# Splitting fp32 weights by whole 128x2048 buffers in a two-layer decoder trunk

## The chip, the cores and the metric

One core of one Trainium2 chip runs the kernel in a single launch. The metric is device time in microseconds. The engines are called as in the profile: PE is TensorE, DVE is VectorE, ACT is ScalarE, POOL is GpSimd, SP is SyncE; PEld is TensorE's weight load, and a trailing q (SPq, ACTq, POOLq) names the queue on which an engine issues DMAs.

## The reference

A decoder trunk of two layers on 256 tokens of width 1024, all in fp32. Each layer is

```python
h = h + 0.5 * swiglu(rmsnorm(h, ffn1_norm[i]), ffn1_w_gate[i], ffn1_w_up[i], ffn1_w_down[i])   # hidden 2816
h = h + mixer_i(rmsnorm(h, mix_norm[i]))      # layer 0: differential attention, layer 1: Mamba-2 SSD
h = h + memory_cross_attention(rmsnorm(h, xa_norm[i]), mem, xa_mem_norm[i], xa_w_q[i], xa_w_kv[i], xa_w_o[i])
h = h + 0.5 * swiglu(rmsnorm(h, ffn2_norm[i]), ffn2_w_gate[i], ffn2_w_up[i], ffn2_w_down[i])
...
def swiglu(h, w_gate, w_up, w_down):
    return (jax.nn.silu(h @ w_gate) * (h @ w_up)) @ w_down
```

and a last RMSNorm follows. The memory of the cross-attention is 256 tokens of width 1024, normalised and projected anew in each layer. There are four FFNs, and with the projections of the mixers and the cross-attention nearly all the work is products of 256 tokens with weight matrices that are read once from DRAM.

## The kernel before, in words

**Products in three parts.** An fp32 product runs as three TensorE products of a reduced type, fp32r. Each operand is split into a high part (the value cast to fp32r) and a low part (value minus high part), and `mm3` adds x_hi·w_hi (line 262), x_hi·w_lo (263) and x_lo·w_hi (264) into one PSUM bank. For a weight the high part `whi` is a cast on ACT (line 224) and the low part `wlo` a subtract on DVE (line 225), which needs whi. So the first matmul on a piece of weight can go when the cast is done, the second when the subtract is done.

**Weights.** A class `W` loads 1 MB, four k-tiles of 128 rows by 512 columns (128x2048 in SBUF), by one DMA on SP's queue (line 161) into the pool `wp` of eight buffers. `Pair` (line 176) does so for two matrices side by side. `Sum` forms the sum of two weight tiles in place: on DVE (line 203), or by an accumulating DMA that POOL issues (line 199).

**Granules.** A `Gran` is the part of such a buffer that is split at once: two k-tiles of 512 columns, that is one half of a buffer, 128x1024. Its whi and wlo come from the pool `hp`, four buffers of 1024 each. `ready` and `use` split granules in the order in which PE will use them, two ahead (`AHEAD`) of the one in use; a buffer in hp is free when the matmuls on its granule are done.

**Units, sevens and hosts.** `wide` makes a unit that multiplies all 1024 rows with a block of 512 columns, in four granules. `stream` gives the same as single steps. `seven` multiplies a 2x2 arrangement of weight tiles with seven products in place of eight, after Strassen; four of the seven are on sums of weight tiles (x1 to x4) with sums of activations (`s_hi`, `s_lo`). Each of the seven has two granules of six matmuls each. In `ffn_hidden` the remaining steps (`gate`, `up`, `gateup`, `down`'s `out`) are hosts; `share` puts them between the seven products by a list of counts: so many hosts ahead of the first product, so many ahead of the second, and so on. `weave` makes one unit of it.

**Order.** The first two units, the first `gate` and the first `up`, are written out by hand for PE, DVE, ACT and SP, as is PE's order in the SSD stage. Elsewhere a scheduler orders the instructions of each engine. `Pipe` holds work with a due time in microseconds of PE's work (`pipe.after(us, f)`), and issues it when PE's program has come so far.

**Small work.** `gs` is silu of gate times up: ACT at line 787, DVE at line 804. `turn` transposes it (`htp`) and splits it into `hid_hi` (ACT, 857) and `hid_lo` (DVE, 858), the activations of `down`. Results of a seven are copied from PSUM as `p` (ACT, 823). During the first FFN DVE also works out the rope tables (`rope_tables`, lines 735 to 763) in small operations of 64 columns.

**Memory.** `mem` is loaded and normalised once in the first FFN, transposed on PE, and kept in SBUF as `memt`, eight tiles of 128x256. For each layer `MemKV.prep` scales and splits it into `mh` and `ml` (lines 457 and 459), and `MemKV.mix` makes the scaled tiles `my` (line 1074), from which `combine` forms the sums for the sevens of the value projection. Layer 1's preparation falls into the end of the SSD stage, whose output y is scaled, transposed (`ty`) and split into `y_hi` on ACT.

Of the kernel before, what the change touches and what calls it, by code (L numbers as in the profile page):

```python
# [57 lines left out]
def trunk(ctx, tc, a, out):  # L58
# [1 line left out]


    const = ctx.enter_context(tc.tile_pool(name="const", bufs=1))
    wp = ctx.enter_context(tc.tile_pool(name="wp", bufs=8))
    hp = ctx.enter_context(tc.tile_pool(name="hp", bufs=4))
    xp = ctx.enter_context(tc.tile_pool(name="xp", bufs=8))
    sp = ctx.enter_context(tc.tile_pool(name="sp", bufs=28))
    wk = ctx.enter_context(tc.tile_pool(name="wk", bufs=7))
# [4 lines left out]
    def slot(name, dt=F32):  # L72
        return sp.tile([P, 512], dt, name=name, tag="s")
# [4 lines left out]
    def small_ps(name):  # L78
        return pacc.tile([P, 512], F32, name=name, tag="acc")
# [28 lines left out]
    class Pipe:  # L108
        def __init__(self):
            self.t = 0.0  # L110
            self.q = []
# [93 lines left out]
    class Gran:  # L205


        def __init__(self, k0, nk, *parts, eng=None):
            self.k0, self.nk, self.parts, self.eng = k0, nk, parts, eng or nc.vector
            self.hi = None  # L210

        def split(self):
            if self.hi is not None:
                return
            hi = hp.tile([P, 1024], F32R, name="whi", tag="hi")
            lo = hp.tile([P, 1024], F32R, name="wlo", tag="lo")
            ncol = sum(n for _, _, n in self.parts)
            self.hi, self.lo = (t[:, :self.nk * ncol].rearrange("p (k c) -> p k c", c=ncol) for t in (hi, lo))
            o = 0
            for w, c0, n in self.parts:  # L220
                w.load()
                src = w.t[:, self.k0 - w.k0:self.k0 - w.k0 + self.nk, c0:c0 + n]
                hv = self.hi[:, :, o:o + n]
                nc.scalar.copy(hv, src)  # L224
                self.eng.tensor_tensor(self.lo[:, :, o:o + n], src, hv.bitcast(F32), op=ALU.subtract)  # L225
                o += n

    grans = []
# [12 lines left out]
            yield g  # L241

    def run_units():
        for gs, _ in units:
            for g in gs:
                g.at = len(grans)
                grans.append(g)
        E = mybir.EngineType
        with tc.manual_schedule(engines={E.PE, E.DVE, E.Activation, E.SP}):
            begin(first_norm)  # L250
            for gs, f in units[:2]:
                f(*gs)
        for gs, f in units[2:written[0]]:
            f(*gs)
        with tc.manual_schedule(engines={E.PE}):
            for gs, f in units[written[0]:written[1]]:
                f(*gs)
        for gs, f in units[written[1]:]:
            f(*gs)
# [316 lines left out]
    def v2(t, j=2):  # L576
        return t.rearrange("p (j t) -> p j t", j=j)
# [67 lines left out]
    lqk2 = lqk  # L645
    lqk = lqk.rearrange("p (k d) -> p k d", k=4)
    subln = cols0[:, KT:KT + 1]
    memt = [const.tile([P, S], F32, name=f"mem{j}") for j in range(KT)]
    mcol = const.tile([P, 16], F32, name="mcol")
    mnat = [[None, None], [None, None]]  # L650
    cols1 = const.tile([P, P], F32, name="cols1")
# [36 lines left out]
    def mem_prep():  # L688
# [12 lines left out]
        def turn(j):  # L701
            ps = small_ps("tin")
            for t in range(2):
                nc.tensor.transpose(ps[:, t * P:(t + 1) * P], mnat[t][j // 4][:, (j % 4) * P:(j % 4 + 1) * P], ident)
            nc.scalar.copy(memt[j], ps[:, :S])
        for j in range(KT):
            pipe.after(6.0 + 1.0 * j, lambda j=j: turn(j))


    def mem_stage():  # L710
# [67 lines left out]
    def ffn_hidden(nm, l, norm, fin, tail, extra=None):  # L778
# [95 lines left out]

        def part(half, ps):
# [181 lines left out]
    class MemKV:  # L1057


        def __init__(self, l):  # L1060
# [4 lines left out]
            self.x = []  # L1065
            self.s = [None] * 4

        def mix(self):
            y = [slot("my") for _ in range(KT // 2)]

            def full(p):
                for j in range(2):
                    k = 2 * p + j
                    nc.scalar.activation(v2(y[p])[:, j, :], memt[k], AF.Copy, scale=self.g[:, k:k + 1])
            for p in range(KT // 2):
                pipe.after(1.4 * p, lambda p=p: full(p))
            combine(y, self.s, [7.0 + 1.6 * i for i in range(8)])

        def k_split(self, c):
            self.ks[c] = split2(self.k[c], "mk")  # L1080

        def prep(self):
            self.x.clear()
            for j in range(KT):
                if j % 2 == 0:
                    mh, ml = slot("mh", F32R), slot("ml", F32R)
                xh, xl = (m[:, j % 2 * S:(j % 2 + 1) * S] for m in (mh, ml))
                split_act(xh, xl, memt[j], self.g[:, j:j + 1])
                self.x.append((xh, xl))

        def k_units(self, then=None, cs=(0, 2)):
            def fin(c):
# [584 lines left out]
```

## Time and profile before

| | us |
|---|---|
| median of 3 runs | 1260.77 |
| lowest, highest | 1260.51, 1260.87 |
| the profiled execution | 1260.69 |
| its span, first to last instruction | 1258.9 |

Mean granted TensorE clock 0.998. The rows below show one execution. A line of the timeline gives the start in us from the span's begin, the duration, the engine, the source line, the operation, out<-in, the shapes and the count, and in brackets the engine's idle time ahead of it and who ended it. Where a row stands for several instructions (x2, x4), its duration is that of all. The duration of a queued instruction overlaps with that of the one behind it, so what an instruction takes from an engine is read from the starts.

### The profile page before, as it was taken

The page shows a single profiled execution, that of the slowest core. Times are in us where ns is not written, and L with a number is a line of the kernel's source. Part 1 is how long each engine was busy: PE and PEld are TensorE (multiplying, and loading weights), DVE is VectorE, ACT ScalarE, POOL GpSimd, SP SyncE. Part 2 cuts the span into 40 slices and gives each one's busy share as a digit, 9 for nine tenths or more (in the row PEclk, how much of TensorE's full clock was granted, in tenths as well). Part 3 has the DMA queues.
Part 4 walks back from the last instruction along what each step waited for, and adds up shares of the span by engine and source line. Part 5 has one row for each costly group of instructions (what it writes and reads, how often), then busy time and mean ns, then how long its engine had stood idle before and what let it go on. Part 6 is the DMA issues. An engine that isn't in the chain of part 4 may idle for free.

```text
span 1258.9 us, 18179 instructions
## 1 busy us (share of the span) xinstructions
PE 1248.6 (99%) x6751; PEld 1070.7 (85%) x6751; DVE 1056.7 (84%) x1451; ACT 878.0 (70%) x1395; POOL 161.7 (13%) x139
## 2 busy tenths in 40 slices
PE   9999999999999999999999999999999999999997
PEld 6887888788998888888888889999998898888886
DVE  6988867887787998988898976788899887899886
ACT  6676764676676876767776756777777775877673
POOL 1101002201101011101111000022232100011100
PEclk9999999999999999999999999999999999999999
DMA  9979975345776698985899966665634786489961
GB/s 335 281 205 283 319 240 183 118 144 150 209 226 168 168 264 270 267 268 167 219 273 265 289 228 214 205 186 168 201 135 135 189 245 177 159 235 276 261 215 34
DMA packets 158316, 269.79 MB, mean 214 GB/s; under 512 B 6890, under 2 KB 43411, under 8 KB 158227
## 3 DMA queue, kind: packets, MB, share of 16 engines
q1 hardware_dynamic: 137744, 229.75, 53.6%
q0 software_dynamic: 19744, 38.28, 17.8%
q8 instruction: 53, 0.87, 0.3%
q10 hardware_dynamic: 738, 0.59, 0.1%
q14 instruction: 37, 0.30, 0.1%
HBM read 267.52 MB, written 1.08 MB: 213 GB/s over the span
## 4 chain that ended last, share of the span: by engine, by line
PE 91%; DVE 4%; DMA 2%; ACT 1%; issue 1%; POOL 0%; POOLq 0%; DVEq 0%; ACTq 0%
PE out L263 9%; PE out L264 8%; PE out L262 8%; PE seven L264 8%; PE seven L263 8%; PE seven L262 8%; DVE wlo L225 2%; PE xs L264 2%; PE xs L262 1%; PE xs L263 1%; DMA w<-in_ffn_w_gate_dram 1%; PE up L263 1%; PE up L264 1%; PE up L262 1%; PE htp L854 1%; PE mk L262 1%
## 5 line engine op out<-in xcount | busy, mean ns | idle before, releaser
L225 DVE TENSOR_TENSOR wlo<-w,whi 128x1024 fp32r<-128x1024 f32 (+2 forms) x532 | 641.0, 1219 | 136.2 <-ACT whi L224 126.7
L224 ACT CAST whi<-w 128x1024 fp32r<-128x1024 f32 (+2 forms) x534 | 552.3, 1040 | 261.9 <-PE out L264 102.5
L262 PE MATMUL out<-whi,hid_hi 128*128 128x512 f32 x336 | 131.4, 394 | 0.5 <-ACT whi L224 0.5
L263 PE MATMUL out<-wlo,hid_hi 128*128 128x512 f32 x336 | 131.3, 391 | 0.4 <-DVE wlo L225 0.3
L264 PE MATMUL out<-whi,hid_lo 128*128 128x512 f32 x336 | 131.0, 390 | 0.0
L262 PE MATMUL seven<-whi,s_hi 128*128 128x512 f32 x272 | 107.7, 396 | 0.4 <-ACT p L823 0.4
L263 PE MATMUL seven<-wlo,s_hi 128*128 128x512 f32 x272 | 106.1, 390 | 0.0
L264 PE MATMUL seven<-whi,s_lo 128*128 128x512 f32 x272 | 106.1, 390 | 0.0
L203 DVE TENSOR_TENSOR w<-w 128x2048 f32<-128x2048 f32 x32 | 73.2, 2286 | 5.7 <-DMA w<-in_ffn_w_gate_dram 5.6
L199 POOL DMA_DIRECT2D w<-in_ffn_w_up_dram x30 | 36.5, 1241 | 310.5 <-DVE wlo L225 273.7
L263 PEld LDWEIGHTS out<-wlo,hid_hi 128*128 128x128 f32 x336 | 63.2, 188 | 14.7 <-DVE wlo L225 2.1
L262 PEld LDWEIGHTS out<-whi,hid_hi 128*128 128x128 f32 x336 | 63.0, 188 | 13.3 <-ACT whi L224 0.8
L264 PEld LDWEIGHTS out<-whi,hid_lo 128*128 128x128 f32 x336 | 63.1, 188 | 13.2
L262 PE MATMUL seven<-whi,xh 128*128 128x512 f32 x180 | 70.1, 389 | 0.0
L264 PE MATMUL seven<-whi,xl 128*128 128x512 f32 x180 | 70.0, 389 | 0.0
L263 PE MATMUL seven<-wlo,xh 128*128 128x512 f32 x180 | 70.0, 389 | 0.0
L199 POOL DMA_DIRECT2D w<-in_ffn_w_gate_dram x30 | 36.9, 1467 | 221.7 <-DVE w L203 76.2
L264 PEld LDWEIGHTS seven<-whi,s_lo 128*128 128x128 f32 x272 | 51.1, 188 | 10.8
L262 PEld LDWEIGHTS seven<-whi,s_hi 128*128 128x128 f32 x272 | 51.1, 188 | 10.5 <-ACT p L823 0.8
L263 PEld LDWEIGHTS seven<-wlo,s_hi 128*128 128x128 f32 x272 | 51.1, 188 | 9.7
L262 PEld LDWEIGHTS seven<-whi,xh 128*128 128x128 f32 x180 | 33.8, 188 | 7.1
L263 PEld LDWEIGHTS seven<-wlo,xh 128*128 128x128 f32 x180 | 33.8, 188 | 7.1
(398 smaller groups left out, 3018.4 us busy)
## 6 DMA issues: line engine op xcount, KB each, us to landing
w<-in_ffn_w_up_dram SPq DMA_DIRECT2D x40, 1024.0 KB, 7.2
w<-in_ffn_w_down_dram SPq DMA_DIRECT2D x40, 1024.0 KB, 8.6
w<-in_ffn_w_gate_dram SPq DMA_DIRECT2D x38, 1024.0 KB, 7.1
w<-in_ssd_w_in_dram SPq DMA_DIRECT2D x24, 1024.0 KB, 5.4
w<-in_xa_w_kv_dram SPq DMA_DIRECT2D x16, 1024.0 KB, 5.1
w<-in_ffn_w_gate_dram POOLq DMA_DIRECT2D x30, 512.0 KB, 9.1
w<-in_ffn_w_up_dram POOLq DMA_DIRECT2D x30, 512.0 KB, 7.4
w<-in_da_w_in_dram SPq DMA_DIRECT2D x12, 1024.0 KB, 5.2
```

Of the source, the lines that this page charges most:

```text
L199: nc.gpsimd.dma_start(self.t[:, k:k + 2, :], w.src[r0:r0 + 2 * P, w.c0:w.c0 + w.n] .rearrange("(k p) c -> p k c", p=P), accum_op=ALU.add)
L203: nc.vector.tensor_tensor(self.t, self.l.t, w.t, op=ALU.add)
L224: nc.scalar.copy(hv, src)
L225: self.eng.tensor_tensor(self.lo[:, :, o:o + n], src, hv.bitcast(F32), op=ALU.subtract)
L262: nc.tensor.matmul(o, lhsT=lh, rhs=rh, start=start, stop=False, skip_group_check=onto)
L263: nc.tensor.matmul(o, lhsT=lh, rhs=rl, start=False, stop=False, skip_group_check=onto)
L264: nc.tensor.matmul(o, lhsT=ll, rhs=rh, start=False, stop=stop, skip_group_check=onto)
L854: nc.tensor.transpose(tp[:, j, t * P:(t + 1) * P], us[t][:, (i + j) * P:(i + j + 1) * P], ident)
```

## The change

Four edits go together.

- **Whole buffers.** `Group` joins granules. Two neighbouring halves of a whole 512-column buffer are split by one cast of 128x2048 (new line 252) and one subtract of 128x2048 (new line 253); the two granules then are views of the pair. Other granules of one unit share a buffer of 2048 but are split one by one as before (new lines 265 and 266). Of 520 splits of 128x1024, 430 become 215 pairs and 90 stay.
- **Pools.** hp has three buffers of 2048 each for whi and for wlo in place of four of 1024. wp has seven buffers in place of eight.
- **Counts.** Hosts stand between the seven products in twos, as whole pairs. In the first FFN the counts for its three column blocks change as the diff shows; in the others, five of the seven products stand in a row at the seam of two blocks.
- **Memory in DRAM.** `memt` is a DRAM tile. Two transposed tiles at a time are copied to SBUF and written by a DMA on ACT's queue. `prep` and `mix` each read four times 256 KB back on ACT's queue ahead of use (`fetch`, new line 1120); the scaling in `mix` starts 5 us later, that in `prep` 4 us later, and the sums in `mix` 5 us later.

```diff
-    wp = ctx.enter_context(tc.tile_pool(name="wp", bufs=8))
-    hp = ctx.enter_context(tc.tile_pool(name="hp", bufs=4))
+    wp = ctx.enter_context(tc.tile_pool(name="wp", bufs=7))
+    hp = ctx.enter_context(tc.tile_pool(name="hp", bufs=3))
...
+        def whole(self, other):
+            w, c0, n = self.parts[0]
+            return (self.parts == other.parts and len(self.parts) == 1 and (c0, n) == (0, 512)
+                    and self.nk == other.nk == 2 and other.k0 == self.k0 + 2)
...
+    class Group:
+        def take(self, g, unit):
+            a = self.gs[-1]
+            if len(self.gs) == 1 and a.whole(g):
+                self.merged = True
+            elif unit != a.unit or self.merged or self.n + g.size() > 2048 or a.parts[0][2] == g.parts[0][2] == 512 and a.nk > 1:
+                return False
+            self.gs.append(g)
+            self.n += g.size()
+            return True
+
+        def split(self, g):
+            if self.t is None:
+                self.t = [hp.tile([P, 2048], F32R, name=n, tag=n) for n in ("whi", "wlo")]
+            if self.merged:
+                a, b = self.gs
+                w = a.parts[0][0]
+                w.load()
+                hi, lo = (t.rearrange("p (k c) -> p k c", c=512) for t in self.t)
+                src = w.t[:, a.k0 - w.k0:a.k0 - w.k0 + 4, :]
+                nc.scalar.copy(hi, src)
+                nc.vector.tensor_tensor(lo, src, hi.bitcast(F32), op=ALU.subtract)
+                for x, k in ((a, 0), (b, 2)):
+                    x.hi, x.lo = hi[:, k:k + 2, :], lo[:, k:k + 2, :]
                 return
...
-    memt = [const.tile([P, S], F32, name=f"mem{j}") for j in range(KT)]
+    memt = dram.tile([P, KT * S], F32, name="memt")
...
+            mt = slot("mt")
+            nc.scalar.copy(v2(mt), ps)
+            nc.scalar.dma_start(memt[:, 512 * i:512 * i + 512], mt)
...
-        five, six = [1, 0, 1, 0, 2, 0, 1], [1, 1, 1, 0, 2, 0, 1]
...
-            counts = {2: [5, 1, 1, 0, 2, 1, 1], 3: [1, 1, 1, 1, 2, 1, 1], 4: [1, 1, 1, 0, 2, 1, 1]}
+            counts = {2: [4, 2, 2, 0, 2, 2, 0], 3: [2, 0, 2, 0, 2, 2, 0], 4: [2, 0, 2, 0, 2, 0, 0]}
...
-            counts = {1: six, 2: five, 3: six, 4: five}
+            counts = {c: [2, 0, 2, 0, 2, 0, 0] for c in (1, 2, 3)}
+            counts[4] = [0, 0, 2, 0, 2, 0, 0]
...
+        def fetch(self):
+            y = [slot("my") for _ in range(KT // 2)]
+            for p in range(KT // 2):
+                nc.scalar.dma_start(y[p], memt[:, 512 * p:512 * p + 512])
+            return y
...
-                pipe.after(1.4 * p, lambda p=p: full(p))
-            combine(y, self.s, [7.0 + 1.6 * i for i in range(8)])
+                pipe.after(5.0 + 1.4 * p, lambda p=p: full(p))
+            combine(y, self.s, [12.0 + 1.6 * i for i in range(8)])
...
+            for p in range(KT // 2):
+                pipe.after(4.0 + 1.0 * p, lambda p=p: cut(p))
```

How this moves the instructions shows in the lists of what each engine gets, in its order. First DVE at the start, between the norm's statistics (`nsum`, `msq`) and the first sums of activations (`sraw`); the splits here are those of the first `up` and, behind it, of `gateup`. Before:

```order
L517 TENSOR_TENSOR nsum<-nss 128x2
L464 TENSOR_SCALAR msq<-nsum 128x2
L225 TENSOR_TENSOR wlo<-w,whi 128x1024 x2
L560 TENSOR_TENSOR y<-xh,xl 128x256 x2
L225 TENSOR_TENSOR wlo<-w,whi 128x1024
L560 TENSOR_TENSOR y<-xh,xl 128x256 x2
L225 TENSOR_TENSOR wlo<-w,whi 128x1024
L560 TENSOR_TENSOR y<-xh,xl 128x256 x4
```

The same place in the changed kernel:

```order
L562 TENSOR_TENSOR nsum<-nss 128x2
L509 TENSOR_SCALAR msq<-nsum 128x2
L253 TENSOR_TENSOR wlo<-w,whi 128x2048
L605 TENSOR_TENSOR y<-xh,xl 128x256 x2
L253 TENSOR_TENSOR wlo<-w,whi 128x2048
L605 TENSOR_TENSOR y<-xh,xl 128x256 x6
```

The first split of `up` now is that of four k-tiles; in ACT's list five casts of 128x1024 at this place have become three of 128x2048. Next DVE behind it, where `gateup` ends and the first product of a seven stands ahead of `gate`'s second column block. Before:

```order
L486 TENSOR_TENSOR s_lo<-sraw,s_hi 128x512
L481 TENSOR_TENSOR sraw<-y 128x256 x2
L225 TENSOR_TENSOR wlo<-w,whi 128x1024
L486 TENSOR_TENSOR s_lo<-sraw,s_hi 128x512
L203 TENSOR_TENSOR w<-w 128x2048
L804 SCALAR_TENSOR_TENSOR gs<-gateup,rcol,gs 128x256 x2
L225 TENSOR_TENSOR wlo<-w,whi 128x1024 x3
L858 TENSOR_TENSOR hid_lo<-htp,hid_hi 128x512
L225 TENSOR_TENSOR wlo<-w,whi 128x1024
```

In the changed kernel (row 40 of DVE's list is the last but one here):

```order
L907 TENSOR_TENSOR hid_lo<-htp,hid_hi 128x512
L253 TENSOR_TENSOR wlo<-w,whi 128x2048
L907 TENSOR_TENSOR hid_lo<-htp,hid_hi 128x512
L853 SCALAR_TENSOR_TENSOR gs<-gateup,rcol,gs 128x256
L531 TENSOR_TENSOR s_lo<-sraw,s_hi 128x512
L853 SCALAR_TENSOR_TENSOR gs<-gateup,rcol,gs 128x256
L531 TENSOR_TENSOR s_lo<-sraw,s_hi 128x512
L253 TENSOR_TENSOR wlo<-w,whi 128x2048
L203 TENSOR_TENSOR w<-w 128x2048
```

Two `s_lo` have moved behind the `gs` of `gateup`, and the split behind them is a whole pair. Last ACT near the end of the SSD stage, where the memory is prepared for layer 1 (`mh`, `my`) and the y chain ends (`junk` is the square of y with its sum, then y is scaled). Before:

```order
L457 ACTIVATE mh<-mem_108,cols_111 128x256
L457 ACTIVATE mh<-mem_109,cols_111 128x256
L224 CAST whi<-w 128x1024
L1074 ACTIVATE my<-mem_102,cols_111 128x256
L1074 ACTIVATE my<-mem_103,cols_111 128x256
L1476 ACTIVATE y<-y,yrc 128x256 x2
L224 CAST whi<-w 128x1024
L1472 ACTIVATE junk,yss<-y 128x256 x2
```

In the changed kernel:

```order
L1120 DMA my<-memt 128x512 x4
L1532 ACTIVATE junk,yss<-y 128x256 x2
L502 ACTIVATE mh<-my,cols_104 128x256 x4
L252 CAST whi<-w 128x2048
L1120 DMA my<-memt 128x512 x4
L502 ACTIVATE mh<-my,cols_104 128x256 x2
L1532 ACTIVATE junk,yss<-y 128x256 x2
L1536 ACTIVATE y<-y,yrc 128x256 x2
L502 ACTIVATE mh<-my,cols_104 128x256 x2
L1129 ACTIVATE my<-my,cols_104 128x256 x2
```

Eight DMA issues stand in ACT's list, and the `mh` behind them wait for the reads.

More of the change, by code (lines that the diff above doesn't have):

```diff
@@ L210, in __init__, with size @@
             self.hi = None
-        def split(self):
-            if self.hi is not None:
+        def size(self):
+            return self.nk * sum(n for _, _, n in self.parts)
+        def whole(self, other):
+            w, c0, n = self.parts[0]
+            return (self.parts == other.parts and len(self.parts) == 1 and (c0, n) == (0, 512)
+                    and self.nk == other.nk == 2 and other.k0 == self.k0 + 2)
+        def split(self):
+            if self.hi is None:
+                self.group.split(self)
@@ new lines, in trunk, with __init__ @@
+    class Group:
+        def __init__(self, g):
+            self.gs, self.n = [g], g.size()
+            self.merged = False
+            self.t = None
+        def take(self, g, unit):
[20 more added lines that the diff above has]
+                    x.hi, x.lo = hi[:, k:k + 2, :], lo[:, k:k + 2, :]
@@ L214, in split @@
                 return
[L215 to L218, printed above, removed]
+            ncol = sum(n for _, _, n in g.parts)
+            o = sum(x.size() for x in self.gs[:self.gs.index(g)])
+            g.hi, g.lo = (t[:, o:o + g.size()].rearrange("p (k c) -> p k c", c=ncol) for t in self.t)
@@ L219, in split @@
             o = 0
-            for w, c0, n in self.parts:
+            for w, c0, n in g.parts:
                 w.load()
-                src = w.t[:, self.k0 - w.k0:self.k0 - w.k0 + self.nk, c0:c0 + n]
-                hv = self.hi[:, :, o:o + n]
+                src = w.t[:, g.k0 - w.k0:g.k0 - w.k0 + g.nk, c0:c0 + n]
+                hv = g.hi[:, :, o:o + n]
                 nc.scalar.copy(hv, src)
-                self.eng.tensor_tensor(self.lo[:, :, o:o + n], src, hv.bitcast(F32), op=ALU.subtract)
+                g.eng.tensor_tensor(g.lo[:, :, o:o + n], src, hv.bitcast(F32), op=ALU.subtract)
@@ L243, in run_units @@
     def run_units():
-        for gs, _ in units:
+        for i, (gs, _) in enumerate(units):
             for g in gs:
-                g.at = len(grans)
+                g.at, g.unit = len(grans), i
+                if not grans or not grans[-1].group.take(g, i):
+                    g.group = Group(g)
+                else:
+                    g.group = grans[-1].group
                 grans.append(g)
@@ L699, in mem_prep, with turn @@
                 nc.scalar.activation(mnat[t][c], mnat[t][c], AF.Copy, scale=mcol[:, t:t + 1])
[L701 to L707, printed above, removed]
+        def turn(i):
+            ps = v2(small_ps("tin"))
+            for j in (2 * i, 2 * i + 1):
+                for t in range(2):
+                    nc.tensor.transpose(ps[:, j % 2, t * P:(t + 1) * P], mnat[t][j // 4][:, (j % 4) * P:(j % 4 + 1) * P],
+                                        ident)
+            mt = slot("mt")
+            nc.scalar.copy(v2(mt), ps)
+            nc.scalar.dma_start(memt[:, 512 * i:512 * i + 512], mt)
+        for i in range(KT // 2):
+            pipe.after(6.0 + 2.0 * i, lambda i=i: turn(i))
     def mem_stage():
@@ L1066, in __init__ @@
             self.s = [None] * 4
+        def fetch(self):
[3 more added lines that the diff above has]
+            return y
         def mix(self):
-            y = [slot("my") for _ in range(KT // 2)]
+            y = self.fetch()
             def full(p):
@@ L1073, in full @@
                     k = 2 * p + j
-                    nc.scalar.activation(v2(y[p])[:, j, :], memt[k], AF.Copy, scale=self.g[:, k:k + 1])
+                    nc.scalar.activation(v2(y[p])[:, j, :], v2(y[p])[:, j, :], AF.Copy, scale=self.g[:, k:k + 1])
             for p in range(KT // 2):
-                pipe.after(1.4 * p, lambda p=p: full(p))
-            combine(y, self.s, [7.0 + 1.6 * i for i in range(8)])
+                pipe.after(5.0 + 1.4 * p, lambda p=p: full(p))
+            combine(y, self.s, [12.0 + 1.6 * i for i in range(8)])
         def k_split(self, c):
@@ L1083, in prep, with cut @@
             self.x.clear()
[L1084 to L1089, printed above, removed]
+            y = self.fetch()
+            def cut(p):
+                mh, ml = slot("mh", F32R), slot("ml", F32R)
+                for j in range(2):
+                    k = 2 * p + j
+                    xh, xl = v2(mh)[:, j, :], v2(ml)[:, j, :]
+                    split_act(xh, xl, v2(y[p])[:, j, :], self.g[:, k:k + 1])
+                    self.x.append((xh, xl))
+            for p in range(KT // 2):
+                pipe.after(4.0 + 1.0 * p, lambda p=p: cut(p))
         def k_units(self, then=None, cs=(0, 2)):
```

## The prediction

> **What bounds the kernel now.** I read the page's busy shares first, then the chain of work that ended last, then what PE waited for. On the page:
>
> ```profile
> PE 1248.6 (99%) x6751; PEld 1070.7 (85%) x6751; DVE 1056.7 (84%) x1451; ACT 878.0 (70%) x1395; POOL 161.7 (13%) x139
> PE 91%; DVE 4%; DMA 2%; ACT 1%; issue 1%; POOL 0%; POOLq 0%; DVEq 0%; ACTq 0%
> ```
>
> TensorE is busy for 99% of the span and carries 91% of the chain. The change touches no matmul, so all it can win is time in which PE stands still for a split. The view of PE's waits says how much that is (line waited for, then us in total, times, longest):
>
> ```profile
> PE warm L597 <- DVE warm L99: 1.5, 1, 1.5
> PE out L262 <- ACT whi L224: 0.5, 1, 0.5
> PE seven L262 <- ACT p L823: 0.4, 1, 0.4
> PE out L263 <- DVE wlo L225: 0.3, 1, 0.3
> ```
>
> The first entry is the warm-up, which the change does not touch. The three others come to 1.2 us. A page counts a pipelined matmul as busy for 0.39 us while the next starts 0.23 us later, so a short stall hides in such a row; at single places I go by starts. Two matmuls in a row, and then a stretch with waits:
>
> ```profile
> 48.54 0.39 PE L262 MATMUL gate<-whi,xh 128*128 128x512 f32 x1
> 48.77 0.39 PE L263 MATMUL gate<-wlo,xh 128*128 128x512 f32 x1
> ```
> ```profile
> 94.05 0.61 PE L262 MATMUL out<-whi,hid_hi 128*128 128x512 f32 x2
> 95.02 0.49 PE L262 MATMUL seven<-whi,s_hi 128*128 128x512 f32 x1 [0.35 <-ACT p L823]
> 95.96 0.73 PE L262 MATMUL out<-whi,hid_hi 128*128 128x512 f32 x2 [0.45 <-ACT whi L224]
> 96.98 0.50 PE L263 MATMUL out<-wlo,hid_hi 128*128 128x512 f32 x1 [0.29 <-DVE wlo L225]
> 97.31 0.40 PE L264 MATMUL out<-whi,hid_lo 128*128 128x512 f32 x1
> ```
>
> From 94.05 to 97.31 PE starts six matmuls. At 0.23 us each they take 1.4 us, they took 3.26: 1.9 us are lost here, while the rope tables' small operations fill DVE. This is the largest split stall of the trace. Smaller ones are quoted below (0.5 us at the start, 0.3 at 508); with a few of 0.2 to 0.5 us, I put what splits cost PE in all at about 4 us. That is the most the change can bring by way of splits.
>
> **The change, part by part. Merged splits.** Before, 520 casts and 520 subtracts have 1024 elements per partition; now 215 pairs of them are one instruction each, and 90 stay. Groups by line and shape, with the mean ns of one behind the busy time:
>
> ```profile
> L225 DVE TENSOR_TENSOR wlo<-w,whi 128x1024 fp32r<-128x1024 f32 x520 | 633.9, 1233 | 131.0 <-ACT whi L224 121.6 <-DMA E<-scr 1.6
> L203 DVE TENSOR_TENSOR w<-w 128x2048 f32<-128x2048 f32 x32 | 73.2, 2286 | 5.7 <-DMA w<-in_ffn_w_gate_dram 5.6
> L224 ACT CAST whi<-w 128x1024 fp32r<-128x1024 f32 x520 | 544.7, 1053 | 260.9 <-PE out L264 102.5 <-PE seven L264 43.3 <-PE gateup L264 15.9
> L857 ACT CAST hid_hi<-htp 128x512 fp32r<-128x512 f32 x44 | 23.9, 590 | 6.9 <-PE htp L854 5.7
> ```
>
> A 2048-wide subtract is not in the trace of before, but a 2048-wide sum is: 2.29 us, against 2 × 1.23 = 2.47. For the cast I extend the line from 590 ns at 512 to 1053 at 1024: about 1.98 us at 2048, against 2.11. By durations DVE would save 215 × 0.18 = 39 us. But durations of queued instructions overlap; the chain gives what one takes from start to start:
>
> ```profile
> 87.53 2.19 DVE w L203
> 91.47 1.13 DVE wlo L225
> ```
>
> 2 × 1.13 − 2.19 = 0.07 us a pair, 215 × 0.07 = 15 us of an engine with 16% of its span free. On the path this is worth nothing unless PE waits for DVE there. The Trainium skill, "VectorE: DVE Perf Modes", section "The TRN2 errata — SBUF-src ops pay a fixed extra latency per instruction", says that one large tile pays the fixed latency once and many small ones pay it for each tile. Its formula agrees with the durations here (2291 ns for 2048 columns). An estimate from it alone, 151 cycles saved for each of 215 pairs, would be 34 us of DVE; the starts, 0.07 us a pair, allow less than half.
>
> What a merge costs is latency: the first matmul on wlo now waits for the whole pair. One place in the hand-ordered part at the start and one behind it show it.
>
> **The start: +2.0 us.** Timeline of before as PE passes from `gate` to the first `up`, and the two chain pieces there:
>
> ```profile
> 17.41 3.89 ACT L224 CAST whi<-w 128x1024 fp32r<-128x1024 f32 x4
> 18.48 2.45 DVE L225 TENSOR_TENSOR wlo<-w,whi 128x1024 fp32r<-128x1024 f32 x2 [0.58 <-ACT whi L224]
> 19.25 0.39 PE L262 MATMUL up<-whi,xh 128*128 128x512 f32 x1
> 19.76 0.19 PEld L263 LDWEIGHTS up<-wlo,xh 128*128 128x128 f32 x1 [0.54 <-DVE wlo L225]
> ```
> ```profile
> 17.50 0.95 ACT whi L224
> 18.48 1.24 DVE wlo L225
> ```
>
> ACT gets to this split at 17.41, DVE has been waiting since 17.9, and PE already waits for the first half's wlo at 19.76. Nothing runs ahead, so the chain cast, subtract, matmul lies bare. With the first pair merged it is 17.41 + 1.98 = 19.39 for whi, + 0.05 + 2.29 = 21.73 for wlo, then the matmul at 21.75: 2.0 us later. PE is never again idle long enough to take it back, so all of it reaches the end. Range +1.7 to +2.2.
>
> **The first product of sevens (about 45 us): +0.6 us, 0 to 1.0.** In the new DVE order the subtract for `gate`'s second column block (row 40) stands behind two `gs` and two `s_lo` that need the end of `gateup` on PE. Before:
>
> ```profile
> 42.87 0.47 ACT L787 ACTIVATE gs<-gateup,rcol 128x256 f32<-128x256 f32 x1 [0.26 <-PE gateup L264]
> 43.05 0.87 DVE L804 SCALAR_TENSOR_TENSOR gs<-gateup,rcol,gs 128x256 f32<-128x256 f32 x2
> 45.33 0.39 PE L262 MATMUL seven<-whi,s_hi 128*128 128x512 f32 x1
> 47.72 0.68 DVE L858 TENSOR_TENSOR hid_lo<-htp,hid_hi 128x512 fp32r<-128x512 f32 x1
> ```
>
> Counted from the end of `gateup` (42.6 before): the cast to gs 0.7, two `gs` by 0.43, two `s_lo` by about 0.6 (the like operation hid_lo has 0.68 with its overlap), the subtract 2.29 and its start: about 5.2 to 5.5 us. PE meanwhile has 12 matmuls of a seven, two of `gate`, one more of the seven and four transposes before it needs wlo: 15 × 0.23 + 0.6 + some 0.5 of evacuation = 4.5 to 4.9. The difference is 0.6; nothing if ACT delivers gs sooner.
>
> **The rope tables (about 95 us): 0, −1.9 to +0.5.** From the two `gs` after `up` to the wlo that `out` waits for, the new DVE order has 2.2 us of sum, four subtracts of 2.2, four hid_lo of 0.6, two `gs` and two `p` at 0.67 and some 35 small operations of 0.13: 20.6 us, against 18.8 us of PE's work. So a stall of 1.8 us in place of 1.9. If the order's slack helps, all of it goes.
>
> **Sevens in a run: +1.0 us, 0 to 3.** The new counts put up to five sevens in a row in the second to fourth FFN. There each split waits until a buffer is released. Before, in the third such stretch:
>
> ```profile
> 504.56 2.29 DVE L203 TENSOR_TENSOR w<-w 128x2048 f32<-128x2048 f32 x1
> 506.30 1.06 ACT L224 CAST whi<-w 128x1024 fp32r<-128x1024 f32 x1 [0.30 <-PE seven L264]
> 506.77 3.49 DVE L225 TENSOR_TENSOR wlo<-w,whi 128x1024 fp32r<-128x1024 f32 x3
> 508.05 0.19 PEld L263 LDWEIGHTS out<-wlo,hid_hi 128*128 128x128 f32 x1 [0.40 <-DVE wlo L225]
> ```
>
> A half is six matmuls, 1.36 us. Four buffers leave three halves, 4.1 us, less 0.3 to release, 1.05 to cast, 1.22 to subtract: a margin of 1.5 us. A sum of 2.2 us ahead in DVE's queue uses it up, and PE waits for wlo, its weight load for 0.40 us, the matmul for some 0.3 of it. With three buffers of a whole pair: 5.46 − 0.3 − 1.98 − 2.29 = 0.9 us. A sum in the way costs up to 0.6 us more. I take one such place in each of the three later FFNs, 0.3 each. One weight buffer fewer works in the same direction: a load is issued about one buffer later, that is by these rows
>
> ```profile
> 460.00:500.00 40.00, 40.00 (x184) 33.14 (x183) 36.94 (x36) 29.59 (x36) 5.39 (x5) 1.00 0.92 267
> w<-in_ffn_w_down_dram SPq DMA_DIRECT2D x40, 1024.0 KB, 8.6
> ```
>
> (the window's last columns are clock, DMA share and GB/s) 1.05 MB / 267 GB/s = 3.9 us of a lead of eight such steps, against a landing of 8.6 us. Seven steps still cover it.
>
> **Transposed memory in DRAM: +0.4 us, 0 to 1.5.** Four writes and 20 reads of 256 KB are new, all issued by ACT; the nearest rows are a transfer of that size and an issue on ACT:
>
> ```profile
> E<-scr SPq DMA_DIRECT2D x16, 256.0 KB, 5.9
> 0.73 0.41 ACTq L87 DMA_DIRECT2D ident<-in_cst_dram  x1
> 940.00:980.00 40.00, 40.00 (x202) 33.73 (x201) 36.53 (x56) 28.45 (x60) 14.39 (x11) 1.00 0.41 123
> ```
>
> 24 × 0.4 to 0.6 = 10 to 14 us of ACT, in stretches where ACT is idle a quarter of the time (28.45 of 40 busy), and 6.3 MB over queues that are 41% busy. The prep is issued 4 us ahead of its use, a little less than a landing of 5.9; behind the waiting `mh` on ACT's queue stand the casts and, at the end of the SSD stage, the y chain. PE has up to 2 us of work there, so I take 0.4 of a lateness of 0.7 to 1.5.
>
> The sum: 2.0 + 0.6 + 0 + 1.0 + 0.4 = +4.0. The profiled execution took 1260.69 us (span 1258.9), 0.08 below the median of the runs shown, so 1260.77 + 4.0 = 1264.8 us.
>
> **The rivals.** *Only the start counts.* The other three positive terms are at the low end of their ranges (zero), and some of the stalls at 95 and 508 go. For it: the waits of before are tiny, and the new counts place hosts so that whole pairs fit. Against it: margins in a run of sevens shrink on paper. 1260.77 + 2.0 − 0 to 1 = 1262.3: no change.
>
> *Relief of DVE and ACT reaches PE.* All 4 us of split stalls go, and so does an excess in the first matmul of each triple. For it: L262 of `out` has a mean of 394 ns against L264's 390 in the page's groups:
>
> ```profile
> L262 PE MATMUL out<-whi,hid_hi 128*128 128x512 f32 x336 | 131.4, 394 | 0.5 <-ACT whi L224 0.5
> L264 PE MATMUL out<-whi,hid_lo 128*128 128x512 f32 x336 | 131.0, 390 | 0.0
> ```
>
> 4 ns × some 900 such triples are 3.6 us. With the start's 2.0 against it: 1260.77 − 4 − 2.5 + 2.0 = 1256.3. Against it: the start is bare and sure, and half of that excess is no wait for a split. The Trainium skill, "Perfetto Trace Analysis", section "Identifying the Most-Contended Engine", holds that matmul busy time is a poor measure and LDWEIGHTS' share a good one; by it 85% would leave room. The trace does not show that room: with nothing to wait for, the step from start to start stays at 0.23 us (48.54 to 48.77).
>
> *Sums ahead of whole pairs.* In the new DVE order 13 of the 32 sums stand directly ahead of a merged subtract. If each costs PE the lost 0.6 us, and if loads land so late (one buffer less) that the sum itself waits 0.3, the price is 13 × 0.9 = 12 us: 1260.77 + 2.0 + 12 = 1275. It decides where the pair behind the sum is the next that PE needs, as at 504 to 508. Against it: the planner loads a sum a seven ahead, and before only one of these places shows a wait of 0.3.
>
> That the merge does not take place can be excluded: the instruction lists have 215 of them.
>
> **How the numbers follow.** Forecast (+2.5 to +8) 0.48, only the start 0.29, sums 0.13, relief 0.10. Two runs of before differ by 0.36 us, and about 0.2% (2.5 us) is what a measurement here can tell from no change: bounds 1258.25 and 1263.3. Relief lies below, "only the start" between. Faster 0.10, same 0.29, slower 0.61. The range leaves out the relief and the worse half of the sums, under 2 in 10, and takes in the ends of the four terms: 1259.5 to 1274.
>
> **What would show it right or wrong.** PE's first `up` on wlo at about 21.75 instead of 19.76 proves the first term; anything near 19.8 refutes it. A wait of `gate` for wlo near 50 us shows the second. Waits of `seven` or `out` for wlo in the four FFNs, just behind a sum, show the fourth, and their total tells the forecast from the third rival. The reads of memory show as ACT waiting for them ahead of `mh`, with PE's `out` late for y_hi near 985. If PE's waits for splits are fewer than before behind the first 60 us, the forecast is wrong, and DVE's and ACT's relief counted for more than I allow.

## The result, and the profile after

The changed kernel takes 1291.14 us (median of 4, 1290.21 to 1293.11) against 1260.67 for the kernel before (1260.51 to 1260.87): ratio 1.0244, interval 1.0226 to 1.0261, some 30 us slower. The forecast had the sign, and about an eighth of the size. The profiled execution took 1290.71 us. The page:

```profile
PE 1261.3 (98%) x6751; PEld 1075.9 (83%) x6751; DVE 1039.0 (81%) x1236; ACT 840.0 (65%) x1176; POOL 168.7 (13%) x139
PE 73%; DVE 10%; DMA 6%; issue 5%; ACT 5%; POOL 1%; DVEq 0%; POOLq 0%; ACTq 0%
L253 DVE TENSOR_TENSOR wlo<-w,whi 128x2048 fp32r<-128x2048 f32 x215 | 492.8, 2295 | 125.1 <-ACT whi L252 123.8
L252 ACT CAST whi<-w 128x2048 fp32r<-128x2048 f32 x215 | 410.9, 1912 | 193.4 <-PE out L309 67.3
```

The merged instructions cost what the rows of before said (2.29 us forecast, 2.295 measured; 1.98 and 1.91), and DVE is busy for 18 us less, ACT for 38 us less. PE's share of the chain has fallen from 91% to 73%: the path now runs for long stretches through DVE and loads. PE's waits:

```profile
PE seven L307 <- DVE p L879: 10.5, 3, 3.6
PE up L308 <- DVE wlo L253: 1.8, 1, 1.8
PE acs L1335 <- issue: 1.8, 1, 1.8
...
PE pcb L1462 <- DVE c L1413: 1.4, 1, 1.4
PE qkt L987 <- ACT p L1030: 1.1, 1, 1.1
```

The largest is new: three times, once in each of the three later FFNs, PE waits 3.5 us for `p`, the subtract on DVE that reads a PSUM bank which the next product of a seven adds to. DVE at the first of these places, with its idle time in brackets, and PE:

```profile
441.79 2.29 DVE L253 TENSOR_TENSOR wlo<-w,whi 128x2048 fp32r<-128x2048 f32 x1 [1.15 <-ACT whi L252]
448.71 2.29 DVE L203 TENSOR_TENSOR w<-w 128x2048 f32<-128x2048 f32 x1 [4.63 <-DMA w<-in_ffn_w_gate_dram]
450.92 0.68 DVE L907 TENSOR_TENSOR hid_lo<-htp,hid_hi 128x512 fp32r<-128x512 f32 x1
451.52 2.28 DVE L253 TENSOR_TENSOR wlo<-w,whi 128x2048 fp32r<-128x2048 f32 x1
453.72 0.68 DVE L907 TENSOR_TENSOR hid_lo<-htp,hid_hi 128x512 fp32r<-128x512 f32 x1
454.32 0.68 DVE L879 TENSOR_TENSOR p<-p,seven 128x512 f32<-128x512 f32 x1
```
```profile
455.15 0.47 PE L307 MATMUL seven<-whi,s_hi 128*128 128x512 f32 x1 [3.58 <-DVE p L879]
```

The first sum of the next column block is at the head of DVE's queue and stands there for 4.6 us, because one of its operands has not landed. Behind it stand four instructions, and the last is what PE needs. The chain gives the load (start, duration):

```profile
436.88 2.30 DVE wlo L253
439.20 9.43 DMA w<-in_ffn_w_gate_dram
448.71 0.10 DVE w L203
```

It is issued when a pair's subtract gives a weight buffer back, and takes 9.4 us.

A wait can cost more than its own length. The windows view behind four waits of PE (of 2.1 us at 19.5, 3.7 at 451, 2.0 at 804.5 and 1.5 at 954), each for some 3.5 us, and behind the second also the 3.5 us after that; the column ahead of the last two is the granted clock:

```profile
22.50:26.50 4.00, 4.00 (x12) 3.13 (x11) 4.00 (x9) 3.06 (x3) 0.00 (x0) 0.57 1.08 366
456.00:459.40 3.40, 3.40 (x10) 2.70 (x9) 3.02 (x2) 1.55 (x1) 0.00 (x0) 0.53 1.07 210
459.50:463.00 3.50, 3.50 (x16) 2.88 (x15) 2.31 (x3) 2.95 (x3) 0.00 (x0) 0.98 1.06 348
807.60:811.00 3.40, 3.40 (x18) 3.35 (x17) 0.46 (x2) 0.97 (x3) 0.00 (x0) 0.53 0.42 153
956.40:960.00 3.60, 3.60 (x21) 2.99 (x20) 3.60 (x5) 1.81 (x5) 0.00 (x0) 1.00 0.84 287
```

In this trace PE runs at about half rate for some 3.4 us behind each wait of 2.0 us and more, and loses about 1.6 us again; behind 1.5 us it does not, and the third row shows it back near full rate. There are five such stretches, 8 us. Each lasts 3.41 us in the trace's clock records, and their starts (22.73, 456.22, 637.12, 807.79 and 1145.71 us) lie whole multiples of that apart. The length of the wait alone does not decide: in `wp8` below, the waits at 19 and 805 us are as long as here, and the granted clock behind both is 1.00. With the waits shown, 16.6 us, the slow stretches make 24 to 25 of the 30; the rest is in smaller waits, of 0.9 us and less, that were not added up.

### The profile page after: what moved, and what is told of

It is laid out like the page before. It is cut to its first block, busy times and chain, and to the rows that moved or that the text cites. A ratio compares the mean times of both kernels' runs of the same rounds, so it can differ in the third digit from the quotient of the medians.

```text
span 1288.9 us, 17535 instructions
## 1 busy us (share of the span) xinstructions
PE 1261.3 (98%) x6751; PEld 1075.9 (83%) x6751; DVE 1039.0 (81%) x1236; ACT 840.0 (65%) x1176; POOL 168.7 (13%) x139
## 4 chain that ended last, share of the span: by engine, by line
PE 73%; DVE 10%; DMA 6%; issue 5%; ACT 5%; POOL 1%; DVEq 0%; POOLq 0%; ACTq 0%
PE out L308 8%; PE out L309 8%; PE out L307 8%; PE seven L308 6%; PE seven L307 6%; PE seven L309 6%; DVE wlo L253 5%; DMA w<-in_ffn_w_gate_dram 4%; ACT whi L252 2%; PE mk L307 1%; PE mk L308 1%; PE mk L309 1%; PE xq L307 1%; PE xq L309 1%; PE xq L308 1%
## 5 line engine op out<-in xcount | busy, mean ns | idle before, releaser
L253 DVE TENSOR_TENSOR wlo<-w,whi 128x2048 fp32r<-128x2048 f32 x215 | 492.8, 2295 | 125.1 <-ACT whi L252 123.8
L252 ACT CAST whi<-w 128x2048 fp32r<-128x2048 f32 x215 | 410.9, 1912 | 193.4 <-PE out L309 67.3
L266 DVE TENSOR_TENSOR wlo<-w,whi 128x1024 fp32r<-128x1024 f32 (+2 forms) x102 | 119.2, 1178 | 29.5 <-ACT whi L265 28.9
L265 ACT CAST whi<-w 128x1024 fp32r<-128x1024 f32 (+2 forms) x104 | 100.8, 983 | 47.3 <-issue 10.2
```

The lines of the kernel that those rows point to most:

```text
L252: nc.scalar.copy(hi, src)
L253: nc.vector.tensor_tensor(lo, src, hi.bitcast(F32), op=ALU.subtract)
L266: g.eng.tensor_tensor(g.lo[:, :, o:o + n], src, hv.bitcast(F32), op=ALU.subtract)
```

## The experiments

Eighteen runs; times are medians, ratios against the kernel before on the same chip, with 95% intervals. Four theories are named in the expectations (a fifth, G, is explained where it stands): **Q**, p stands in DVE's queue behind a sum that waits; **B**, one weight buffer fewer makes the loads late; **L**, a pair takes too long to split; **R**, a pair gives back its weight buffer, and lets an accumulation start, only at its end, which makes the next load land late.

**The parts one by one.** First the kernel before with one part of the change at a time. The counts alone (the new lists of the diff):

> The kernel before with the new host counts alone: halves are split as before, eight weight buffers, memory in SBUF. The list of DVE has the next block's sum ahead of p here too. Theory Q: the queue order comes with the counts, so the three seams wait for p here as well, up to 16 us, about 1270 to 1277; less if eight buffers bring the load earlier. Theory L (the length of a whole pair's chain of sum, cast and subtract is what hurts): halves make it short, 1260 to 1264. Theory B: no buffer is missing, 1260 to 1263.

1264.28 us, 1.0025 (1.0016 to 1.0035): +3.2 us. p stands behind the sum here too, and PE does not wait for it. So the order of the queue is not enough; Q in its plain form is weakened.

```diff
-    wp = ctx.enter_context(tc.tile_pool(name="wp", bufs=8))
+    wp = ctx.enter_context(tc.tile_pool(name="wp", bufs=7))
```

> The kernel before with seven weight buffers instead of eight and nothing else; its order on DVE at the seams is that of before, p ahead of the sum. Theory B: loads go out one buffer later everywhere, sums wait for them, and a good part of the 30 us is here: 1270 to 1285. Theories Q and L: 1261 to 1264, since nothing that PE needs stands behind the sum.

1270.92 us, 1.0074 (1.0058 to 1.0089): +9.8 us. PE's and DVE's waits:

```profile
PE seven L263 <- DVE wlo L225: 7.2, 8, 1.6
```
```profile
DVE w L203 <- DMA w<-in_ffn_w_gate_dram: 25.3, 12, 3.6
```

In the kernel before, DVE's sums wait 5.6 us for these loads in all; with a buffer fewer 25.3. The prediction had counted on seven buffers to cover a landing. The memory in DRAM alone (the hunks of the diff that name `memt`, `fetch` or `cut`):

> The kernel before with the transposed memory in DRAM and nothing else. My forecast of this term: +0.4 us, 0 to 1.5, so about 1261.2. In the changed kernel PE waits 1.8 us more at the transition to the SSD stage's cumulative sums, 1.4 for c near 955 and 1.2 in the attention: if the DMA issues on ACT and the reads cause these, they appear here, 1263 to 1265; if the merged splits in the queues cause them, they don't.

1260.90 us, 0.9999 (0.9990 to 1.0009): nothing. The waits at the cumulative sums and at c are absent, so they belong to the rest of the change.

**The merge.** All of the change but the merge, with the split buffers in three sizes: three, four or six halves (six have the bytes of three pairs). `whole` is never asked, and for four and six the tile has 1024 elements:

```diff
-            if len(self.gs) == 1 and a.whole(g):
+            if False:
```

> The changed kernel with every granule split by itself: counts, seven weight buffers and memory in DRAM stay, the three split buffers hold one half each. Theory L: the latency of the pairs is gone, the start's 2 us and most of the 30 us go, 1262 to 1268, though three halves in place of four may cost some us. Theory B: the seventh buffer still costs, 1280 or more. Theory Q: in this list p stands behind no late sum at the seams, so these 16 us go, 1265 to 1275.

> The changed kernel with every granule split by itself and four buffers of one half, as the kernel before has them: what is left of the change is the counts, memory in DRAM and seven weight buffers. Alone these cost 3.2, 0 and 9.8 us. If they add up: 1274. Then the pairs cost the other 17 us of the change (theories Q and L), and the split-by-itself run with three halves lost 22 us to its missing fourth half. If it is 1285 or more, seven buffers and the new counts make it worse together, and the pairs cost little.

> As the run with four halves, but with six, the same bytes as three whole pairs. If the depth of the split buffers is what decides, 2 to 10 us faster than with four; if the weight buffers decide, the same within 2 us. Against the changed kernel it differs by the merge alone: theories Q and L expect 12 to 17 us less than 1291, theory B the same time.

Three halves: 1296.35 us, 1.0277 (1.0262 to 1.0292). Four: 1271.29, 1.0084 (1.0069 to 1.0099), near the 1274 of the sum of parts. Six: 1268.20, 1.0059 (1.0044 to 1.0074). So at equal bytes the merge costs 23 us. That could be the long instruction or the grouping. The next run keeps the groups and their buffers and splits each pair by two instructions on each engine:

```diff
-                nc.scalar.copy(hi, src)
-                nc.vector.tensor_tensor(lo, src, hi.bitcast(F32), op=ALU.subtract)
                 for x, k in ((a, 0), (b, 2)):
+                    ks = slice(k, k + 2)
+                    nc.scalar.copy(hi[:, ks, :], src[:, ks, :])
+                    nc.vector.tensor_tensor(lo[:, ks, :], src[:, ks, :], hi[:, ks, :].bitcast(F32), op=ALU.subtract)
```

> The changed kernel with the pairs kept as groups (one buffer of 2048, split at one place in the program), but each pair split by two casts and two subtracts of 128x1024 again. Buffers, counts and memory are those of the changed kernel. Theory R and L (the length of one instruction: PE, the weight buffer's release and the accumulations all wait for the last element of 2048): most of the 23 us go, 1266 to 1275, the start's wait is 0.5 us again. Theory G (what costs is the group: three buffers that come free only when twelve matmuls are done): 1285 or more, and the start alone gains.

1269.71 us, 1.0072 (1.0057 to 1.0087): 21.4 us less than the change. The groups are the same, so it is the length of the instruction. PE's waits, and the load and sum at the first seam in its chain:

```profile
PE seven L308 <- DVE p L880: 4.1, 3, 1.7
```
```profile
432.14 4.94 DMA w<-in_ffn_w_gate_dram
440.04 0.61 DVE w L203
```

Counted from the `gate` matmul from which PE runs on without a break in this FFN (407.46 here, 413.67 in the changed kernel), the sum starts at 32.6 us in place of 35.0, and p with it. The 4.94 us of the row are not the whole landing: by the windows view DMA moves 308 GB/s from 437.0 to 439.7 us and nothing from 439.8 on, so the load took some 7.6 us here, against 9.4. The accumulating DMAs that run beside it start earlier too, 21.2 us behind that `gate` matmul in place of 23.1 (changed kernel first):

```profile
436.76 2.47 POOL L199 DMA_DIRECT2D w<-in_ffn_w_up_dram  x2 [22.29 <-DVE wlo L253]
```
```profile
428.62 2.47 POOL L199 DMA_DIRECT2D w<-in_ffn_w_up_dram  x2 [19.58 <-DVE wlo L255]
```

PE's three waits have shrunk from 3.5 us to 1.4 on average and 1.7 at most, with no drop of the clock behind them, and the wait at the first `up` is gone from the list. These places make some 15 of the 21 us; the rest was not located.

**The late load.** The same order on DVE as in the changed kernel, without the accumulating DMAs, so x3 and x4 are incomplete:

```diff
             if self.into == "dma":
-                for k in (0, 2):
-                    r0 = (w.k0 + k) * P
-                    nc.gpsimd.dma_start(self.t[:, k:k + 2, :], w.src[r0:r0 + 2 * P, w.c0:w.c0 + w.n]
-                                        .rearrange("(k p) c -> p k c", p=P), accum_op=ALU.add)
+                pass
```

> The changed kernel without the 60 accumulating DMAs of 512 KB: the tiles of x3 and x4 then hold what x3 and x4 would be added to, so those products are left incomplete. DVE's order at the seams is unchanged, p behind the sum. Theory R (late landing): the load of the next block's sum, 9.4 us now with an accumulation beside it, lands in 5 to 7 us, the sum waits 1 to 2 us in place of 4.7, PE's waits for p shrink from 3.6 to under 1 us and the half-rate matmuls behind them go: 12 to 16 us less, 1275 to 1279 or lower. If the waits stay over 2 us, landing isn't what sets them, 1286 or more.

1269.53 us, 1.0067 (1.0050 to 1.0084). DVE at the same seam, the landing times, and DVE's waits for these loads in all:

```profile
438.47 0.37 SPq L161 DMA_DIRECT2D w<-in_ffn_w_gate_dram  x1
443.72 2.29 DVE L200 TENSOR_TENSOR w<-w 128x2048 f32<-128x2048 f32 x1 [0.39 <-DMA w<-in_ffn_w_gate_dram]
449.33 0.68 DVE L876 TENSOR_TENSOR p<-p,seven 128x512 f32<-128x512 f32 x1
```
```profile
w<-in_ffn_w_gate_dram SPq DMA_DIRECT2D x38, 1024.0 KB, 5.1
```
```profile
DVE w L200 <- DMA w<-in_ffn_w_gate_dram: 5.5, 9, 1.0
```

The load is issued at the same point, 25.5 us behind that `gate` matmul in both kernels, and lands after 5.2 us in place of 9.4; p comes in time though it still stands behind the sum, and PE has no wait for p. This shows the late landing as the cause of the three waits, and the accumulations as what makes it late here. The waits and the slow stretches behind them were 15 to 16 us; where the other 6 of the 21.6 us come from was not located.

**The order of the queue.** All sums kept back to their place in program order:

```diff
-                nc.vector.tensor_tensor(self.t, self.l.t, w.t, op=ALU.add)
+                tc.keep_in_program_order(nc.vector.tensor_tensor(self.t, self.l.t, w.t, op=ALU.add))
```

> The changed kernel with one edit: each sum on DVE (the new line 203) is kept behind all that stands ahead of it in program order on DVE, so that the first sum of the next column block no longer stands ahead of the subtract p of the block in work. Theory Q (queue order): in the three later FFNs PE waits 3.5 to 3.8 us for p, because p stands in DVE's queue behind a sum that waits for its load, and loses 1.6 us more at half rate behind each wait; all three go, 3 x 5.3 = 16 us, time about 1275. Theory B (one weight buffer fewer): the load itself is late, the sum waits just the same, and what waits for it moves from p to the sum's own split: under 5 us gained, 1286 to 1291. Theory L (a whole pair is too long to split): 1289 to 1292, the waits at the seams only change their names.

1314.50 us, 1.0420 (1.0404 to 1.0435). The wait for DVE's `p` (line 879) is gone, and others take its place, above all this one:

```profile
PE seven L307 <- ACT p L872: 11.0, 7, 1.7
```

A sum that is issued late has sum, cast and subtract still ahead of it, 2.3 + 1.9 + 2.3 us, and ACT's copies stand behind the cast that waits. Then only the next block's first sum, loaded and pinned directly behind p:

```diff
                         c12()
+                        if c + 1 in sums:
+                            sums[c + 1].load()
```

> The changed kernel, its first sum of each next column block alone put directly behind p in DVE's order; all other sums stay where they were. Keeping all sums back cost 23 us, because the second sums then came too late; here they don't move. Theory Q (p stands behind a sum that waits for its load): the three waits for p of 3.6 us go and the eight slow matmuls behind each, 3 x 5.3 = 16 us, 1275; the sum then has 13 us until PE needs it. Theory L (pairs are too long): the wait moves to the sum's own split, under 5 us gained. Theory B (buffers): the same, since the load comes no earlier.

1318.19 us, 1.0457 (1.0439 to 1.0474). DVE's list was as intended, and the wait at 451 is gone; but the scheduler now put the next `p` in front of the splits that PE needs:

```profile
DVE p L890 <- PE seven L312: 38.6, 11, 3.8
```

My theory Q, that mending the order returns 16 us, fell: each order tried has some instruction at the head of DVE's queue that waits. That the lateness of the awaited thing decides, and not the order, is what the runs with shorter instructions and without accumulations speak for. With the first pair of `up` in two halves as well:

> The changed kernel with the sum behind p and the first pair of up in two halves. The first pair alone gained 1.1 us of the 2.0 to 3.7 that I expected, since what was gained at 20 us was lost at 46 us and at the seams, where DVE and the loads set the pace. With the seams free I expect 1272 to 1274, that is 1 to 3.5 us less than with the sum behind p alone.

1319.51 us, 1.0465 (1.0449 to 1.0481), nothing gained.

**The start, buffers and counts in the changed kernel.** The first pair of `up` in two halves:

```diff
-            if len(self.gs) == 1 and a.whole(g):
+            if len(self.gs) == 1 and a.whole(g) and not (unit == 1 and a.k0 == 0):
```

> The changed kernel with the first pair of the first up split in two halves as before. My forecast of the start was +2.0 us; the trace has 2.1 us of waiting there and eight matmuls at 0.43 us in place of 0.23 behind it. All theories: the wait goes to 0.5 us or less and the slow matmuls with it, 3.3 to 3.7 us gained, about 1287.5. If the slow matmuls at the start are no consequence of the wait, only 1.6 to 2 us are gained.

1290.00 us, 1.0236 (1.0215 to 1.0257). The wait at 19 us and the slow stretch are gone, but what they cost is lost again at 46 us and later; the total moves by about 1 us, less than the run-to-run scatter.

Eight weight buffers, four small slots fewer:

```diff
-    wp = ctx.enter_context(tc.tile_pool(name="wp", bufs=7))
+    wp = ctx.enter_context(tc.tile_pool(name="wp", bufs=8))
-    sp = ctx.enter_context(tc.tile_pool(name="sp", bufs=28))
+    sp = ctx.enter_context(tc.tile_pool(name="sp", bufs=24))
```

> The changed kernel with eight weight buffers again, paid for by four of the 28 small slots. In DVE's order the sum then stands one place earlier, still ahead of p. Theory B: the load is issued a buffer earlier, some 4 us, which is about the wait of 4.7 us that the sum has now, so the three seams shrink to under 1 us each and the time falls by 12 to 16 us, to 1275 to 1279. Theory Q: the order is what counts; the sum still stands ahead of p, the wait is the landing less what DVE has to do ahead of it; a gain only as far as the load comes earlier, 0 to 10 us. Theory L: 0 to 2 us.

1296.02 us, 1.0278 (1.0262 to 1.0293). PE's waits:

```profile
PE seven L307 <- DVE p L879: 8.6, 3, 3.5
PE pcb L1462 <- DVE c L1413: 5.8, 1, 5.8
```

The three waits have moved to a place some 40 us on, and the one for `c` in the SSD stage has grown from 1.4 to 5.8 us; that may come from the slots, which was not tested. So the merged kernel's cost isn't the eighth buffer alone; what the buffer is worth there stays open. The old counts (the lines on `five`, `six` and `counts` of the change taken back):

> The changed kernel with the host counts of before. Then hosts stand singly between the sevens and can't be merged there; the sevens' pairs still are. In DVE's order p stands ahead of the sum again. Theory Q: the three waits for p go, 16 us, time about 1275, or a little more for splits that come late where singles and pairs alternate. Theory B: the seventh buffer is still missing, 3 us gained at most. Theory L: pairs behind single hosts have less lead than before, PE waits at many places by 0.5 to 1 us, and the time is 1285 or more.

1299.34 us, 1.0313 (1.0294 to 1.0333): PE waits 14.4 us for wlo in sevens, the sums 27.4 for loads. The time is in L's range, but the waits are fewer and longer than L has them: six, up to 4.2 us.

**Which pairs, and depth alone.** Pairs for plain weights only, and for sums only (`isinstance` without `not`), with two buffers of a pair and two of a half:

```diff
-            if len(self.gs) == 1 and a.whole(g):
+            if len(self.gs) == 1 and a.whole(g) and not isinstance(g.parts[0][0], Sum):
...
+                m = 2048 if self.merged else 1024
+                self.t = [hp.tile([P, m], F32R, name=n, tag=n + str(m), bufs=2) for n in ("whi", "wlo")]
```

> The changed kernel with whole pairs only for weights as loaded; the sums x1 to x4 are split in halves. Buffers: two of a pair and two of a half, the same bytes. Theory R (release: a pair gives its weight buffer back, and lets the sum in place or the accumulating DMA start, only when all four k-tiles are split, which makes the next loads late, and the sum that waits for them holds up DVE's queue): if the accumulation onto the second sum's tile is what makes the load late, it starts some 3.7 us earlier with halves, the load lands 1 us earlier or more, and the three seams shrink; 1270 to 1280. If the plain buffers' release is what counts, 1285 or more.

> The complement: whole pairs only for the sums x1 to x4, plain weights in halves, the same buffers as the run before. If the sums' release is what makes the loads late: 1285 or more, the seams wait as in the changed kernel. If the plain buffers are: 1270 to 1280. If both are 1285 or more, two buffers of each kind are too few for either, and the runs tell nothing.

1326.05 us, 1.0511 (1.0491 to 1.0531), and 1437.98, 1.1399 (1.1384 to 1.1415): both above 1285, so the buffers were too few and nothing follows about which pairs cost. Of the kernel before with the memory in DRAM: six split buffers (`hp`, `bufs=6`) with seven weight buffers, and five with eight:

> The kernel before with memory in DRAM, seven weight buffers and six split buffers of a half: old counts, no merge, the bytes of the change. Seven weight buffers with four split buffers cost 9.8 us. With the new counts six in place of four split buffers gained 3.1. If depth makes good for the weight buffer: 1261 to 1266. If the weight buffer decides: 1268 to 1271.

> The kernel before with memory in DRAM and the 8 KB that this frees spent on a fifth split buffer of a half for whi and wlo each; eight weight buffers, old counts, no merge. If depth of the split buffers is worth something where no weight buffer is missing, 1256 to 1260, up to the 4 us that I put on PE's waits for splits; if PE's waits are not set by the depth, 1260.5 to 1262.

1278.98 us, 1.0132 (1.0117 to 1.0148), and 1261.97, 1.0004 (0.9995 to 1.0013). In the first the sums wait 43.0 us for loads, up to 7.0 at a time, and PE waits for p, at 518 us right behind such a sum:

```profile
PE seven L262 <- DVE p L834: 11.9, 6, 3.9
```

So the same wait arises without one merged instruction. That DVE runs further ahead of the loads with six split buffers, and is stopped longer, is a likely reason, not shown. In the second the sums wait 17.9 us and the time is that of before: a sum that waits costs only what PE needs behind it. Depth is worth nothing there. No run beat the kernel before.

## Why the prediction was wrong

**What bounds the kernel.** Nothing speaks against it: the 4 us were an estimate of the most that could be won, and no run came out below the kernel before.

**Durations, DVE's relief.** Right: DVE is busy for 17.7 us less, near the 15 from the starts, and it was without worth, as forecast.

**The start, +2.0.** The wait came as worked out (matmul at 21.65, forecast 21.75), and 1.6 us for the clock on top, which was missing. That it would all reach the end is not borne out: taken away, it returned about 1 us, less than the scatter.

**The first product of sevens, +0.6.** Right: 0.63 us, `gate` waiting for wlo at 50. **Rope tables, 0.** Right in size, by luck: 1.4 us in place of 1.9, but some 6 us later and mostly for `p` on ACT, where a late wlo was forecast. (Of the 1.9 us of before, which the prediction counts as a stall for splits, 0.5 is PE's wait for `p` at 95.02.) **Memory, +0.4.** Alone 0.0 within 0.1%. The lateness is there on ACT and costs PE nothing:

```profile
989.39 0.42 ACT L1532 ACTIVATE junk<-y 128x256 f32<-128x256 f32 x1 [4.20 <-DMA my<-memt]
```

**Sevens in a run, +1.0 (0 to 3).** This step failed. It measured some 15 to 16 us: three waits of 3.5 us and three slow stretches of 1.6. I counted what a sum takes in DVE's queue (2.2 us), but not how long it stands there before it can begin, nor what else stands behind it: I looked for the wait at the pair behind the sum, and it was at p. The sentence in it that failed first is that seven steps of lead still cover a landing: by itself the eighth buffer was worth 9.8 us in the kernel before. The lead counted in buffers says little, since a load is issued when a split gives a buffer back, and lands 5 us later or 9, according to what runs beside it. The latency of a merged split, which the prediction priced at 2.6 us for the start and the first product and at 0.3 us a place in the sevens, also went into this lead: with the rest of the change in place the merge cost 21 to 23 us.

**The rivals.** The third named the mechanism nearest to it, a sum that waits for a load one buffer late, at 0.3 us a place; the sums waited up to 4.7. It had 0.13 and a price of 12. No rival had the clock: a long wait was charged at its length.

What was not in the forecast at all: waits of 1.8, 1.4 and 1.1 us in the SSD stage and the attention. They are absent where counts, buffers or memory were changed alone in the kernel before. The first, at the cumulative sums, is also 1.8 us in `nomerge` and `pair_two`, so the long instruction does not make it. Beyond that their cause was not isolated. That two changes each take back 21 us, shorter instructions and no accumulations, is no contradiction: both bring the same load's landing forward, and one is enough to keep PE's waits under 2 us.

## What to carry to other kernels

Merging instructions on an engine off the path saves that engine's time and lengthens the latency of all that waits for its last element: the consumer, but also the buffer that is given back and the load that waits for it. Look for in-order queues in which an instruction waits for a DMA, and list what stands behind it; changing their order by hand only moved the wait here. A buffer fewer is priced by which load becomes late and who waits, not by the mean lead.

## What the runs showed of the hardware

- In the changed kernel PE's rate halved behind waits of 2.0 us and more: 0.43 us from start to start for 128x512 in place of 0.23, for 3.41 us; granted clock 0.53 to 0.57 in the windows shown. Behind 1.5 us the window has 1.00, and so it has behind two waits of about 2 us in `wp8`. The Trainium skill, "TensorE: Matmul & The Clock Gate", section "Why this matters for your kernels", advises against idle gaps of more than about 3 us. The half rate is what these rows show; the gap ahead of it was shorter at 804.5 us, 2.0 us.
- A 1 MB load of gate weights landed in 5.1 us at the median without accumulating DMAs in the kernel, in 7.5 with them (the row of the changed kernel below), and in 9.4 at the seam, where two had been issued 2.4 us ahead of it.

```profile
w<-in_ffn_w_gate_dram SPq DMA_DIRECT2D x38, 1024.0 KB, 7.5
```
